# Token-major values by transposing DMA instead of TensorE transposes, in a two-layer hybrid block on one core

## The chip, the cores and the metric

The kernel runs on one core of a Trainium2 chip. The metric is the device time of one execution in microseconds (us); lower is better. The core has five engines with queues of their own: TensorE (PE, matrix products), VectorE (DVE), ScalarE (ACT), GpSimd (POOL) and SyncE (SP), which here issues the DMAs. Each engine takes its instructions in the order in which they were written into its queue.

## The reference

Two layers run over 16 meta tokens and 256 input tokens, width 1024. Each layer mixes tokens in three branches and then applies a convolutional feed-forward block.

```python
def mixer(hn, ...):
    proj = (hn @ w_in).astype(F32)
    rq, rk, rv, rg, hq, hf, hi, hg, dq, dk, dv, mg = jnp.split(proj, offs, axis=-1)
    o_ret = retention(rq, rk, rv, rg, valid, pos)              # 4 heads, values rv, 256 wide
    o_hg = hgrn2(hq, hf, hi, hg, lb, valid)                    # 8 heads, values hi, 128 wide
    o_da = diff_attention(dq, dk, dv, lam_p, subln_g, ...)     # 8 heads, values dv, 128 wide
    branches = jnp.stack([o_ret, o_hg, o_da], axis=2)
    y_b = jnp.einsum('blnc,ncd->blnd', branches, w_branch)
    return jnp.sum(jax.nn.sigmoid(mg) * y_b, axis=2) @ w_out

h = h + mixer(rms_norm(h, g1), ...)
h = h + conv_ffn(rms_norm(h, g2), ...)      # twice, then a final rms_norm of h[:, PAD:]
```

What matters here: in each branch the values (rv, hi, dv) are multiplied from the left by a token-by-token matrix, so that product contracts over tokens.

## The kernel before, in words

**Layout.** Activations lie feature-major: 128 features on the partitions, the 272 tokens (T) along the free dimension. A product of the weight stream makes a pair of feature tiles, `[128, 2, 272]`, in PSUM (tile `main`, two buffers). Weights come as 404 chunks of eight 128x128 float32 tiles. For each chunk SP issues a load into `wraw` (three buffers), ScalarE rounds it to `whi` and VectorE subtracts to get `wlo` (four buffers each). One weight tile then takes three matmuls on TensorE: hi x hi, hi x lo, lo x hi (L912 to L914).

**Order of the weight stream.** `ORDER` lists the pairs of one layer. The pairs of values stand in it like this: `hi` 0 and 1 early, then, after `rg`, `rq` and `rk`, `hi` 2 and 3 and `rv` 0 to 3 directly behind one another, then `dv` 0 and 1, and later `dv` 2 and 3. The heads of a branch are spread as small TensorE work between the main matmuls.

**Values.** A pair of values is feature-major, and the heads need it with tokens on the partitions. `values` (L1378) evacuates the pair from PSUM to a tile `vsrc` on ScalarE (or, before the norm is folded in, on VectorE). `to_tokens` (L948) turns the first 256 tokens: four TensorE transposes into a PSUM tile `vt` of the tag `bank`, then two ScalarE copies from there into the token-major tile (`vt` for hi and dv, `rvt` for rv). The last 16 tokens are copied by GpSimd into `tails` and turned separately for all heads in `tail_tokens`. The heads (`ret_tail` L1000, `ret_head` L1015, `hg_outputs`, `da_head`) then multiply with the token-major tiles; in the profile these are the groups `ro<-wts,rvt`, `ho<-at,vt` and `do<-wts,vt`.

**Who sets the order.** Nothing is issued as it is written. Every operation is handed to `_Plan` with a cost and a due time (`plan.key`); `order` simulates the engines with those costs, the number of buffers of each tag, 0.4 us between engines and 2 us for a DMA to land, and emits one fixed order for each engine. Costs are formulas in `_Engine`; for a GpSimd copy of n elements a partition

```python
cost = self.fixed + self.each * n      # pool: 0.04, 0.85e-3
cost += 1.6e-3 * n                     # pool, except memset
```

A weight load is due `LEAD` = 6 us ahead of its matmuls (L40, L632). `_span` (L383) tells which range of a tile an operation touches. `plan.queue(first, last)` adds an edge: `first` comes after `last`. `SLOTS` (L39) is the number of buffers of the tag `slot`, each 4 x 272 float32 wide, which hold most intermediate blocks, the token-major values among them. The tag `vsrc` has two buffers, the tag `acc` in PSUM has two.

Nearly all small operations are recorded through one helper, so most profile rows have its line, L604; they are told apart by their tiles.

Of the kernel before, what the change touches and what calls it, by code (L numbers as in the profile page):

```python
# [12 lines left out]
F32 = mybir.dt.float32  # L13
F32R = mybir.dt.float32r
U8 = mybir.dt.uint8
AF = mybir.ActivationFunctionType
ALU = mybir.AluOpType
PSUM = bass.MemoryType.PSUM
# [2 lines left out]
P = 128  # L21
# [3 lines left out]
T = META + SEQ  # L25
# [10 lines left out]
TAIL = T - 2 * P  # L36
BANK = 512
CHUNK_TILES = 8
SLOTS = 14  # L39
LEAD = 6.0  # L40
MARGIN = 12.0
EARLY = 12.0
# [313 lines left out]
class _Plan:  # L356
# [5 lines left out]
    SWITCH = 1.3  # L362
    SETS = {AF.Exp: "le", AF.Ln: "le", AF.Silu: "silu", AF.Sigmoid: "sigmoid"}

# [18 lines left out]
    def _span(self, ap):  # L383
        step = ap.ap[0][0]
        lo = ap.offset % step
        hi = lo + 1 + sum((n - 1) * abs(s) for s, n in ap.ap[1:])
        if ap.tensor.name in self.psum:

            lo, hi = lo // BANK * BANK, -(-hi // BANK) * BANK
        return ap.tensor.name, lo, hi  # L390

    def add(self, engine, run, cost, outs, ins, func=None):
# [216 lines left out]
class _Weights:  # L609
# [13 lines left out]
    def next(self):  # L623
        c, i = divmod(self.used, CHUNK_TILES)
        self.used += 1
        if i == 0:
# [7 lines left out]
            for p in range(pieces):  # L634
# [5 lines left out]
                for first, outer, inner, dims in _boxes(*mine):  # L640
                    src = self.part(raw, (p * n + first) * P, inner * P, P, outer, inner)
                    to_hi, to_lo = (self.part(t, *x, outer, inner) for t, x in zip((hi, lo), dims))
                    self.act.activation(to_hi, src, AF.Copy)
                    self.dve.tensor_tensor(out=to_lo, in0=src, in1=to_hi.bitcast(F32), op=SUB)
# [19 lines left out]
def _trace(ctx, tc, plan, a, depth, probe):  # L664
    nc = tc.nc
    act = _Engine(plan, nc.scalar, "act", 0.094, 0.833e-3)
    dve = _Engine(plan, nc.vector, "dve", 0.068, 1.042e-3)
    pe = _Engine(plan, nc.tensor, "pe", 0.0, 4 / 2400)
    pool = _Engine(plan, nc.gpsimd, "pool", 0.04, 0.85e-3)
    sync = _Engine(plan, nc.sync, "sp", 0.06, 4 / 360e3)  # L670
# [3 lines left out]
    wp = ctx.enter_context(tc.tile_pool(name="wp", bufs=3))  # L674
    sp = ctx.enter_context(tc.tile_pool(name="sp", bufs=SLOTS))
    gp = ctx.enter_context(tc.tile_pool(name="gp", bufs=3))
    tp = ctx.enter_context(tc.tile_pool(name="tp", bufs=2))
# [6 lines left out]
    def new(pool_, shape, dt, tag, bufs, name):  # L684
        serial[0] += 1
        return plan.tile(pool_, shape, dt, tag, bufs, f"{name}_{serial[0]}")

    def fixed(shape, name, dt=F32):
        return new(cp, shape, dt, name, 1, name)

    def slot(name, dt=F32):
        return new(sp, [P, 4 * T], dt, "slot", SLOTS, name)

    def slot4(name, dt=F32):
        return slot(name, dt).rearrange("p (a t) -> p a t", a=4)
# [4 lines left out]
    def temp(cols, tag, bufs=2):  # L700
        return new(tp, [P, cols], F32, tag, bufs, tag)

    def temp2(tag, bufs=2):
        return temp(2 * T, tag, bufs).rearrange("p (a t) -> p a t", a=2)

    def bank(name):
        return new(bp, [P, 512], F32, "bank", 2, name)

    def acc_bank(name):
        return new(bp, [P, 512], F32, "acc", 2, name)  # L710

    def tt(out, x, y, op):
        dve.tensor_tensor(out=out, in0=x, in1=y, op=op)
# [7 lines left out]
    def pair(t, n=2):  # L721
        return t.unsqueeze(1).to_broadcast([t.shape[0], n, t.shape[1]])
# [19 lines left out]
    ident = const[:, C_IDENT : C_IDENT + P]  # L742
    masks = fixed([P, 5 * 64], "masks", U8)
    lev = masks[:, : 2 * 64]
# [37 lines left out]
    def parameters():  # L782
# [4 lines left out]
        tt(e, raw, pair(mx), SUB)  # L787
        act.activation(e, e, AF.Exp)
        tt(sm, e[:, 0], e[:, 1], ADD)
# [11 lines left out]
        dve.tensor_reduce(out=sl, in_=pr, axis=mybir.AxisListType.X, op=ADD)  # L801
        act.activation(sl, sl, AF.Exp)
        for li in range(DEPTH):
# [7 lines left out]
    def rsqrt(out, ms, scale=1.0):  # L811

        act.activation(out, ms, AF.Ln, bias=eps, scale=scale)
        act.activation(out, out, AF.Exp, scale=-0.5)

# [108 lines left out]
    def evacuate(out, ps):  # L924
        factor = pair(rstd[:, T - ps.shape[2] :])
        if norm.folded:
            act.activation(out, ps, AF.Copy)
        elif norm.adds is pool and norm.pairs == 1:

            act.activation(out, ps, AF.Copy)  # L930
            plan.key += 2.0
            pool.tensor_tensor(out=out, in0=out, in1=factor, op=MUL)
        else:
            tt(out, ps, factor, MUL)
# [12 lines left out]

    def to_tokens(src, vt, e):  # L948

        pt = bank("vt").rearrange("p (f c e) -> p f c e", f=2, c=2)  # L950
        for f in range(2):
            for c in range(2):
                pe.transpose(pt[:, f, c, :], src[:, f, c * P : (c + 1) * P], ident)
        for f in range(2):
            act.activation(vt[:, :, e + f * P : e + (f + 1) * P], pt[:, f], AF.Copy)

    def tail_tokens(tails):

# [6 lines left out]
    def inverse(r, sq, n):  # L965

        pool.partition_all_reduce(r, sq, P, ReduceOp.add)
        rsqrt(r, r, 1.0 / n)
# [11 lines left out]
    for li in range(depth):  # L980
# [16 lines left out]
        st = {}  # L997


        def ret_tail():  # L1000

            q, k = (st[n][:, :, 2 * P :].unsqueeze(1).to_broadcast([P, 2, 4, TAIL]) for n in ("rq", "rk"))
            ks = temp(P, "tw")
            twice = lambda t: t.rearrange("p (e h t) -> p e h t", e=2, h=4)
            pool.tensor_copy(twice(ks), k)
            s1 = bank("s1")[:, :P]
            pe.matmul(twice(s1), ks, q, start=True, stop=True)
            w = temp(P, "tw")
            tt(w, s1, const[:, C_DECT : C_DECT + P], MUL)
            o = acc_bank("ro")[:, :P]  # L1010
            pe.matmul(o, st["rvs"], w, start=True, stop=True)
            st["ro"] = temp(P, "tw")
            act.activation(st["ro"], o, AF.Copy)

        def ret_head(hd):  # L1015
            q, k, vt, gate = st["rq"], st["rk"], st["rvt"], st["rg"]
            if hd == 0:
                st["dec"] = slot4("dec")
                sync.dma_start(st["dec"].rearrange("p h t -> p (h t)"), a["dec"])
            dec = st["dec"][:, hd, :]  # L1020

            s1 = bank("s1")
            a1 = temp(T + P + TAIL, "wts")
            parts = ((0, t0, t0, dec[:, t0:]), (P, P, T, dec[:, : P + TAIL]))
            for k0, q0, at, _ in parts:
                pe.matmul(s1[:, at : at + T - q0], k[:, hd, k0 : k0 + P], q[:, hd, q0:], start=True, stop=True)
                plan.hold(a1)
            for _, q0, at, by in parts:
                tt(a1[:, at : at + T - q0], s1[:, at : at + T - q0], by, MUL)
            os = [acc_bank("ro") for _ in range(2)]  # L1030
            sq = temp2("sum", 1)
            for e in range(2):
                o = os[e]
                ec = slice((hd * 2 + e) % 4 * P, (hd * 2 + e) % 4 * P + P)
                v = vt[(hd * 2 + e) // 4]
                pe.matmul(o[:, t0:T], v[:, 0, ec], a1[:, t0:T], start=True, stop=False)
                pe.matmul(o[:, P:T], v[:, 1, ec], a1[:, T : T + P + TAIL], start=False, stop=True)
            for e in range(2):
                i = (e * 4 + hd) * TAIL
                tt(os[e][:, 2 * P : T], os[e][:, 2 * P : T], st["ro"][:, i : i + TAIL], ADD)  # L1040
            for e in range(2):
                act.activation(sq[:, e, t0:], os[e][:, t0:T], AF.Square)
            tt(sq[:, 0, t0:], sq[:, 0, t0:], sq[:, 1, t0:], ADD)
            r = temp(T, "hr")
            inverse(r[:, t0:], sq[:, 0, t0:], 2 * P)
            for e in range(2):
                g = gate[:, hd * 2 + e, t0:]
                y = temp(T, "ho")[:, t0:]
                tt(y, os[e][:, t0:T], r[:, t0:], MUL)
                tt(g, y, g, MUL)  # L1050
# [326 lines left out]

        def values(ps, vt, e):  # L1378

            src = temp2("vsrc")  # L1380
            evacuate(src, ps)
            plan.key += 2.0
            to_tokens(src, vt, e)
            return src
# [57 lines left out]
        for name, j in ORDER:  # L1442
# [4 lines left out]
            elif name in ("+hga", "+hgb"):  # L1447
                b = "ab".index(name[3])
# [3 lines left out]
            elif name in ("+daa", "+dab"):  # L1452
                b = "ab".index(name[3])
# [7 lines left out]
            elif name[0] == "*":  # L1461
# [4 lines left out]
                else:  # L1466
                    t = st["rg" if n == "b0" else "hg"]
# [4 lines left out]
            two = slice(2 * (j % 2), 2 * (j % 2) + 2)  # L1472
            both = slice(2 * j, 2 * j + 2)
            if name in BASE:
                lo = 0 if name in FULL else t0
# [17 lines left out]
                elif name in ("dq", "dk"):  # L1493
                    t = block(f"{name}{j // 2}")
# [3 lines left out]
                elif name == "rv":  # L1498
# [3 lines left out]
                    src = values(ps, st["rvt"][j // 2], (j % 2) * 2 * P)  # L1502
# [4 lines left out]
                elif name in ("hi", "dv"):  # L1507
                    n = name[0] + "v"
                    b = j // 2
# [5 lines left out]
                    src = values(ps, st[f"{n}t{b}"], (j % 2) * 2 * P)  # L1515
# [6 lines left out]
                else:  # L1522
                    t = block(f"{name}{j // 2}")
# [21 lines left out]
            elif name == "wo":  # L1545
                hi, lo = st["yhi"], st["ylo"]
# [8 lines left out]
            elif name == "fi":  # L1555
# [10 lines left out]
                c = temp2("two_b")  # L1566
# [8 lines left out]
                c = c[:, :, first:]  # L1575
# [6 lines left out]
            else:  # L1582
                hi, lo = st["ghi"], st["glo"]
# [35 lines left out]
```

## Time and profile before

| | |
|---|---|
| median of 3 runs | 1308.54 us (1308.46 to 1308.67) |
| profiled execution, its own time | 1308.31 us |
| its span, first to last instruction | 1306.5 us |
| granted TensorE clock | 0.999 |
| DMA | 219.06 MB, mean 168 GB/s |

In a group's row stand the line, the engine, the operation, what it writes and reads, the shapes and the count; behind the first bar the busy time in us and the mean ns of one; behind the second the idle time of the engine before it and what ended that. In a row of waits stand who waited for whom, the us in total, how many times and the longest. Timeline rows begin with the start and the length in us.

### The profile page before, as it was taken

To read this page: it belongs to the slowest core of one execution; us is meant where nothing else is said; L and a number is where in the kernel's file an instruction comes from. 1 tells how busy PE (TensorE), PEld (TensorE's weight loads), DVE (VectorE), ACT (ScalarE), POOL (GpSimd) and SP (SyncE) were. 2 spreads that over 40 slices of the span, in tenths; PEclk is the share of its full clock that TensorE was granted. 3 is DMA by queue.
4 is the path that set the end of the run, shared out by engine and by line. 5 is a ranking of instruction groups with operands and counts; after the bars stand their busy time and mean duration, and the time that the engine had idled before them with its cause. 6 is when DMAs were issued, how large, how long until landed. Compare 5 with 4: busy or idle time off the path is not lost.

```text
span 1306.5 us, 28679 instructions
## 1 busy us (share of the span) xinstructions
PE 1294.6 (99%) x11774; PEld 1265.6 (97%) x11774; DVE 958.4 (73%) x1589; ACT 800.5 (61%) x1328; POOL 168.6 (13%) x204
## 2 busy tenths in 40 slices
PE   9999999999999999999999999999999999999998
PEld 9999999999999999999999999999999999999986
DVE  7675777698586789886575767876985867898843
ACT  6846454756576567666456564657565765776643
POOL 5001111222122020000030011012130220200000
PEclk9999999999999999999999999999999999999999
DMA  7644543443534545555555445444445445465553
GB/s 271 200 148 161 169 156 130 162 146 123 184 136 158 181 156 178 189 167 185 175 177 188 164 148 177 148 147 160 146 144 180 139 162 202 145 208 196 200 189 111
DMA packets 60755, 219.06 MB, mean 168 GB/s; under 512 B 6864, under 2 KB 6992, under 8 KB 60624
## 3 DMA queue, kind: packets, MB, share of 16 engines
q1 hardware_dynamic: 60336, 216.71, 49.0%
q8 instruction: 92, 1.51, 0.5%
q10 hardware_dynamic: 288, 0.52, 0.1%
q14 instruction: 39, 0.32, 0.1%
HBM read 216.16 MB, written 1.05 MB: 166 GB/s over the span
## 4 chain that ended last, share of the span: by engine, by line
PE 92%; DVE 5%; issue 1%; ACT 1%; DMA 0%; SPq 0%; DVEq 0%; ACTq 0%
PE main L912 27%; PE main L914 27%; PE main L913 26%; PE fo L1420 2%; PE fo L1419 2%; PE fo L1418 2%; DVE two_b L604 1%; PE lev L1096 1%; DVE two_a L604 1%; DVE wlo L604 1%; PE ds L1280 1%; PE vt L604 1%; PE ro L604 1%; PE ho L604 1%; PE do L604 1%
## 5 line engine op out<-in xcount | busy, mean ns | idle before, releaser
L912 PE MATMUL main<-xh,whi 128*128 128x272 f32 (+1 forms) x2368 | 682.0, 288 | 0.0
L913 PE MATMUL main<-xl,whi 128*128 128x272 f32 (+1 forms) x2368 | 672.5, 284 | 1.5 <-DVE xl L604 1.5
L914 PE MATMUL main<-xh,wlo 128*128 128x272 f32 (+1 forms) x2368 | 673.1, 284 | 0.9 <-DVE wlo L604 0.5
L604 DVE TENSOR_TENSOR wlo<-wraw,whi 128x1024 fp32r<-128x1024 f32 (+1 forms) x411 | 501.9, 1227 | 202.9 <-ACT whi L604 202.2
L604 ACT ACTIVATE whi<-wraw 128x1024 fp32r<-128x1024 f32 (+1 forms) x411 | 427.6, 1043 | 244.5 <-PE main L913 167.1
L914 PEld LDWEIGHTS main<-xh,wlo 128*128 128x128 f32 x2368 | 445.8, 188 | 2.7 <-DVE wlo L604 2.7
L913 PEld LDWEIGHTS main<-xl,whi 128*128 128x128 f32 x2368 | 446.1, 188 | 2.2 <-DVE xl L604 1.9
L912 PEld LDWEIGHTS main<-xh,whi 128*128 128x128 f32 x2368 | 446.1, 188 | 1.0
L604 DVE SCALAR_TENSOR_TENSOR two_b<-main,small,two_b 128x256 f32<-128x256 f32 (+2 forms) x144 | 65.3, 486 | 24.8 <-ACT two_b L604 23.1
L604 POOL PARTITION_ALL_REDUCE hr<-hsq x36 | 67.5, 1886 | 117.0 <-ACT hsq L604 116.2
L604 POOL TENSOR_TENSOR y<-h,rstd 128x272 f32<-128x272 f32 x32 | 34.6, 1112 | 318.1 <-ACT rstd L604 318.1
L604 ACT ACTIVATE two_b<-main,small 128x272 f32<-128x272 f32 (+1 forms) x72 | 37.3, 566 | 24.3 <-PE main L914 23.3
L912 PE MATMUL main<-ghi,whi 128*128 128x272 f32 x176 | 51.0, 290 | 0.0
L913 PE MATMUL main<-glo,whi 128*128 128x272 f32 x176 | 50.6, 287 | 0.0
L914 PE MATMUL main<-ghi,wlo 128*128 128x272 f32 x176 | 50.3, 286 | 0.0
L604 POOL COPY tails<-vsrc 128x32 f32<-128x32 f32 x32 | 10.1, 330 | 225.0 <-ACT vsrc L604 224.9
L912 PE MATMUL main<-b0hi,whi 128*128 128x272 f32 (+1 forms) x128 | 37.9, 296 | 0.0
L912 PE MATMUL main<-b1hi,whi 128*128 128x272 f32 (+1 forms) x128 | 37.8, 296 | 0.0
L912 PE MATMUL main<-yhi,whi 128*128 128x272 f32 (+1 forms) x128 | 36.4, 284 | 0.0
L914 PE MATMUL main<-yhi,wlo 128*128 128x272 f32 (+1 forms) x128 | 36.4, 284 | 0.0
L913 PE MATMUL main<-b1lo,whi 128*128 128x272 f32 (+1 forms) x128 | 36.3, 284 | 0.0
L914 PE MATMUL main<-b1hi,wlo 128*128 128x272 f32 (+1 forms) x128 | 36.3, 284 | 0.0
(236 smaller groups left out, 1915.9 us busy)
## 6 DMA issues: line engine op xcount, KB each, us to landing
wraw<-in_w SPq DMA_DIRECT2D x402, 512.0 KB, 3.3
h<-in_h SPq DMA_DIRECT2D x4, 272.0 KB, 5.3
dec<-in_dec SPq DMA_DIRECT2D x2, 544.0 KB, 4.2
wraw<-in_w SPq DMA_DIRECT2D x4, 256.0 KB, 4.5
const<-in_const SPq DMA_DIRECT2D x1, 937.0 KB, 6.1
gain<-in_gl SPq DMA_DIRECT2D x1, 512.0 KB, 5.5
out<-y ACTq DMA_DIRECT2D x2, 256.0 KB, 3.0
out<-y SPq DMA_DIRECT2D x2, 256.0 KB, 2.9
```

The costliest lines, as they stand in the source:

```text
L604: self.plan.add(self.name, lambda: f(*args, **kw), cost, outs, ins, args[2] if method == "activation" else None)
L912: nc.tensor.matmul(o, wh, hi, start=first, stop=False)
L913: nc.tensor.matmul(o, wh, lo, start=False, stop=False)
L914: nc.tensor.matmul(o, wl, hi, start=False, stop=last)
L1096: nc.tensor.matmul(o, keys, x, start=True, stop=True)
L1280: nc.tensor.matmul(ss[m][:, at : at + nk], q[half, hd, q0 : q0 + P], k[half, hd, :nk], start=True, stop=True)
L1418: nc.tensor.matmul(o, gh, wh, start=False, stop=False)
L1419: nc.tensor.matmul(o, gl, wh, start=False, stop=False)
L1420: nc.tensor.matmul(o, gh, wl, start=False, stop=end)
```

## The change

`to_tokens` no longer uses TensorE, PSUM or ScalarE. It views the float32 values as pairs of 16-bit halves. Two GpSimd copies part the halves into two planes of 128 x 512 (tile `apart`), two DMAs on SP's queue with `transpose=True` turn the four 128x128 blocks of each plane (tile `turned`), and two GpSimd copies join the halves in the token-major tile. Both new tiles are of the tag `vsrc`, which gets four buffers instead of two; `SLOTS` goes from 14 to 13. `_span` learns to count 16-bit views in float32 units. An edge makes the first value matmul of each half of a retention head come after the ScalarE copy of `ret_tail`. The transposes of the last 16 tokens (`tail_tokens`) stay as they are.

```diff
-SLOTS = 14
+SLOTS = 13
...
+        if ap.dtype == U16:
+            lo, hi = lo / 2, hi / 2
         return ap.tensor.name, lo, hi
...
     def to_tokens(src, vt, e):
 
-        pt = bank("vt").rearrange("p (f c e) -> p f c e", f=2, c=2)
-        for f in range(2):
-            for c in range(2):
-                pe.transpose(pt[:, f, c, :], src[:, f, c * P : (c + 1) * P], ident)
-        for f in range(2):
-            act.activation(vt[:, :, e + f * P : e + (f + 1) * P], pt[:, f], AF.Copy)
+        def planes(name):
+            return new(tp, [P, 4 * T], U16, "vsrc", 4, name)[:, : 8 * P].rearrange("p (i x) -> p i x", i=2)
+
+        apart, turned = planes("apart"), planes("turned")
+        halves = lambda t, i: t.bitcast(U16).rearrange("p a (x two) -> p a x two", two=2)[:, :, :, i]
+        for i in range(2):
+            pool.tensor_copy(apart[:, i].rearrange("p (c f x) -> p c f x", c=2, f=2),
+                             halves(src[:, :, : 2 * P], i).rearrange("p f (c x) -> p c f x", c=2))
+        for i in range(2):
+            sync.dma_start(turned[:, i].rearrange("p (b x) -> p b x", x=P), apart[:, i], transpose=True)
+        for i in range(2):
+            pool.tensor_copy(halves(vt[:, :, e : e + 2 * P], i), turned[:, i].rearrange("p (c x) -> p c x", c=2))
...
             act.activation(st["ro"], o, AF.Copy)
+            st["rot"] = plan.ops[-1]
...
                 pe.matmul(o[:, t0:T], v[:, 0, ec], a1[:, t0:T], start=True, stop=False)
+                plan.queue(plan.ops[-1], st["rot"])
...
-            src = temp2("vsrc")
+            src = temp2("vsrc", 4)
             evacuate(src, ps)
```

More of the change, by code (lines that the diff above doesn't have):

```diff
@@ L15 @@
 U8 = mybir.dt.uint8
+U16 = mybir.dt.uint16
 AF = mybir.ActivationFunctionType
```

## The prediction

> **What bounds the kernel now.** I read the page of the profile first: span, busy times, the chain that ended last.
>
> ```profile
> span 1306.5 us, 28679 instructions
> PE 1294.6 (99%) x11774; PEld 1265.6 (97%) x11774; DVE 958.4 (73%) x1589; ACT 800.5 (61%) x1328; POOL 168.6 (13%) x204
> PE 92%; DVE 5%; issue 1%; ACT 1%; DMA 0%; SPq 0%; DVEq 0%; ACTq 0%
> ```
>
> TensorE is busy through 99% of the span and is 92% of the chain. A microsecond taken off TensorE is therefore a microsecond off the end, as long as nothing that feeds it comes late. VectorE has a quarter of the span free, GpSimd nearly all of it. Next, the waits, first of TensorE alone, then of ScalarE's weight conversion:
>
> ```profile
> PE wt L1306 <- DVE two_a L604: 1.6, 4, 0.5
> PE main L913 <- DVE xl L604: 1.5, 2, 1.1
> PE warm L604 <- POOL eps L604: 1.0, 1, 1.0
> PE do L604 <- DVE tw L604: 0.8, 1, 0.8
> PE main L914 <- DVE wlo L604: 0.5, 2, 0.3
> ACT whi L604 <- PE main L913: 167.1, 141, 3.0
> ACT whi L604 <- DMA wraw<-in_w: 17.2, 14, 3.4
> ```
>
> TensorE hardly waits, and after its warm-up it waits for VectorE. The conversion of raw weights (whi, wlo) stood 141 times because TensorE had not yet freed one of its four buffers and only 14 times for a load. So the weights usually run ahead as far as their buffers let them, and that is the cover for much of what follows.
>
> **TensorE's gain.** The change removes 24 groups of four transposes (four pairs each of hi, rv and dv in two layers). One group in the timeline of TensorE (columns: start, length), then the groups of its kind, and ScalarE's evictions behind them:
>
> ```profile
> 160.14 0.29 PE L913 MATMUL main<-xl,whi 128*128 128x272 f32 x1
> 160.26 0.29 PE L914 MATMUL main<-xh,wlo 128*128 128x272 f32 x1
> 160.39 0.60 PE L604 MATMUL vt<-const,vsrc 128*128 128x128 f32 x4
> 160.74 0.37 PE L912 MATMUL main<-xh,whi 128*128 128x272 f32 x1
> 160.95 0.29 PE L913 MATMUL main<-xl,whi 128*128 128x272 f32 x1
> ...
> L604 PE MATMUL vt<-const,vsrc 128*128 128x128 f32 x96 | 15.7, 276 | 0.0
> L604 ACT ACTIVATE vt<-vt 128x256 f32<-128x256 f32 x32 | 10.8, 381 | 3.1 <-PE vt L604 2.6
> L604 ACT ACTIVATE rvt<-vt 128x256 f32<-128x256 f32 x16 | 5.3, 382 | 6.0 <-PE vt L604 6.0
> ```
>
> The 276 ns of one transpose overlap, so I go by starts. From 160.26 to 160.95 pass 0.69 us, where two ordinary steps (0.125 us, as from 160.14 to 160.26) take 0.25: the group costs 0.44 us. From its start to the next main matmul it is 0.35; the other 0.09 is lost in switching, and stays where other small TensorE work stands beside the group. So 24 groups are worth between 24 x 0.35 = 8.4 and 24 x 0.44 = 10.6 us. Most groups stand between main matmuls, so I take 10.0. ScalarE loses 10.8 + 5.3 = 16.1 us of evictions; it isn't the bound, so that counts for nothing.
>
> **GpSimd's copies.** Each group gets four copies of 512 16-bit elements a partition, 96 in all; no such copy is in the trace. The nearest rows (instructions on one tile; min/median/max ns):
>
> ```profile
> L604 POOL COPY dt<-two_a x32: 197/198/1129, 292.8 to 1047.6; 128x16 f32<-128x16 f32 x32
> L604 POOL COPY tw<-rk x2: 289/540/792, 171.6 to 824.2; 128x128 f32<-128x128 f32 x2
> L604 POOL COPY tails<-vsrc x32: 204/212/1052, 74.2 to 991.0; 128x32 f32<-128x32 f32 x32
> L604 POOL TENSOR_TENSOR y<-h,rstd x32: 757/972/1764, 21.6 to 1128.7; 128x272 f32<-128x272 f32 x32
> ```
>
> By minima, 112 elements more cost 92 ns, 0.82 ns each; 512 elements cost 197 + 496 x 0.82 = 604 ns. The upper end goes by the two-input y row: 757 x 512 / 272 = 1.42 us. I take 0.60, because these are copies with one input; that they are 16-bit with a stride of two is what could move it. GpSimd gets 96 x 0.60 = 58 us more, and has room.
>
> The cost is not GpSimd's own time. The maxima above, four to five times the minima, have a partner on VectorE. Eight GpSimd instructions in a row, what VectorE did meanwhile, and wlo overall:
>
> ```profile
> 475.24 8.47 POOL L604 TENSOR_TENSOR y<-h,rstd 128x272 f32<-128x272 f32 x8 [66.64 <-ACT rstd L604]
> 476.14 1.70 DVE L604 TENSOR_TENSOR wlo<-wraw,whi 128x1024 fp32r<-128x1024 f32 x1 [0.23 <-ACT whi L604]
> 478.51 1.77 DVE L604 TENSOR_TENSOR wlo<-wraw,whi 128x1024 fp32r<-128x1024 f32 x1 [0.67 <-ACT whi L604]
> L604 DVE TENSOR_TENSOR wlo<-wraw,whi x411: 418/1224/2189, 5.8 to 1290.6; 128x1024 fp32r<-128x1024 f32 x132, 128x512 fp32r<-128x512 f32 x4, 128x256 fp32r<-128x256 f32 x1
> ```
>
> Beside them wlo takes 1.70 and 1.77 us instead of 1.22, and the eight take 8.47 instead of 8 x 0.757 = 6.1. Both engines pay: they take turns. The Trainium skill, "SBUF — State Buffer", section "Who interferes with whom", states the rule: a VectorE instruction with two SBUF inputs and a GpSimd instruction that reads SBUF share a read port, held for a whole instruction, and the later one stands still. The trace agrees (1.70 against 1.22), and the rule speaks against this change, since wlo is such an instruction.
>
> So I charge VectorE with every copy in full, 0.60 us, as the upper end, and nothing as the lower. Where has it no room for that? Busy time by stretch:
>
> ```profile
> core 0: us, PE busy (x) PEld busy (x) DVE busy (x) ACT busy (x) POOL busy (x), PEclk, DMA share, GB/s
> 73.00:91.00 18.00, 18.00 (x378) 17.25 (x376) 13.17 (x22) 10.27 (x21) 0.51 (x3) 1.00 0.43 148
> 155.00:202.00 47.00, 47.00 (x754) 45.74 (x753) 35.07 (x64) 28.16 (x55) 6.44 (x9) 1.00 0.50 170
> 333.00:352.00 19.00, 19.00 (x157) 19.00 (x156) 10.39 (x10) 12.72 (x22) 2.02 (x8) 1.00 0.52 177
> 805.00:862.00 57.00, 57.00 (x841) 55.70 (x840) 45.61 (x80) 31.79 (x59) 4.78 (x10) 1.00 0.48 163
> ...
> 484.00:512.00 28.00, 27.26 (x217) 26.61 (x216) 27.86 (x53) 20.96 (x37) 0.00 (x0) 1.00 0.39 134
> ```
>
> The second and fourth stretches hold six groups in a row (the last two of hi, four of rv). There 24 copies want 14.5 us, and VectorE has 11.9 and 11.4 us free: 2.6 + 3.1 = 5.7 us too much. Stretches with two groups want 4.8 us and have 4.8 (first) to 8.6 free. When VectorE is full, TensorE does notice: in the last stretch VectorE works 27.86 of 28 us and TensorE idles 0.74. The weight buffers absorb a part, so between 0 and 5.7 I take 3.0 us.
>
> **The DMAs.** There are 48 more, two a group, on SP's queue; each waits for a GpSimd copy, and the weight loads are queued behind it. None is in the trace; its nearest rows are:
>
> ```profile
> wraw<-in_w SPq DMA_DIRECT2D x402, 512.0 KB, 3.3
> h<-in_h SPq DMA_DIRECT2D x4, 272.0 KB, 5.3
> q1 hardware_dynamic: 60336, 216.71, 49.0%
> L604 SPq DMA_DIRECT2D wraw<-in_w x406: 327/328/716, 1.6 to 1283.7; - x136
> ```
>
> A plane has 128 KB. By these rows it takes 0.33 us of issue and lands 3.3 to 5.3 us later; the engines that move data are half idle. Two planes delay a weight load by under 1 us of issue plus the wait for a copy, against loads meant to start 6 us ahead (LEAD): nothing on the path. The Trainium skill, "VectorE: DVE Perf Modes", section "The three transpose paths", gives 1309 ns for a 128x128 16-bit block by DMA and 390 ns on TensorE, and advises TensorE where PSUM will do. By it eight blocks in turn take 10.5 us a group, an estimate, beside TensorE's 0.44 here; no run so far shows a transposing DMA.
>
> Are the values late? They were turned long before they were used (start of first and last):
>
> ```profile
> L604 ACT ACTIVATE rvt<-vt x16: 377/383/386, 174.6 to 852.3; 128x256 f32<-128x256 f32 x16
> L604 PE MATMUL ro<-wts,rvt x64: 284/332/395, 209.3 to 894.8; 128*128 128x144 f32 x32, 128*128 128x272 f32 x16, 128*128 128x258 f32 x16
> ```
>
> From 174.6 to 209.3 there are 35 us. The new path takes 4 x 0.60 for the copies, up to 0.85 us before each (1052 - 204 of tails) and a landing of at most 5.3 after 0.66 of issue: 11.8 us. So latency costs nothing. The four vsrc buffers serve three tiles a group; a third group needs them two spacings later (47 / 6 x 2 = 15.7 us), also longer than 11.8. The joining copies wait on GpSimd for the landing, with the heads' reductions queued behind them, and ScalarE's hr behind those. One slot tile less costs nothing: along the old program's order of issue I count at most 12 held of 14. The new edge (retention's value matmuls after the copy of ro) splits one burst of small TensorE work in each layer: 2 x 0.09 = 0.2 us.
>
> **Sum.** The profiled execution took 1308.31 us (span 1306.5), 0.23 under the median of 1308.54. 1308.31 - 10.0 + 3.0 + 0.2 = 1301.5 profiled, 1301.7 as a median. Its own range is 1297.9 (all 10.6, nothing given back) to 1306.0 (8.4 gained, 5.9 given back).
>
> **Rivals.**
> - *VectorE becomes the bound in the two long stretches; slower.* All 48 copies there hold VectorE up, nothing is absorbed, and a 16-bit copy costs more than 0.60. The loss is 48 d - 23.3 us: it equals the gain of 10.0 at d = 0.69, and at 0.9 it is 19.9, so 1308.5 + 9.9 + 0.2 = 1318.6 us. For it: wlo at 1.77 and the small margin in d. Against it: the copy minima, and the buffers ahead.
> - *SP's queue is held by the transposes; slower.* If SP stands for a whole landing, 2 x 5.3 = 10.6 us a group and 0.9 for its weight loads exceed the spacing of 7.8 by 3.7; six in a row make 22 us, less 6 of lead 16, in both layers 32: 1308.5 + 32 - 10 = 1330.5 us. For it: nothing shows how a transpose is issued, and the skill's 10.5 us would fit. Against it: a load holds SP for 0.33 us whatever its landing.
> - *The gain is eaten.* Joins that stand in GpSimd's queue hold up head reductions, and with them small TensorE work that stands in a fixed order: 24 groups x 0.4 us give the 10 back, 1308.5. For it: GpSimd works in order. Against it: TensorE's waits now are few, and the only one for GpSimd is in its warm-up.
>
> **Numbers.** Forecast 0.55; VectorE 0.20; SP 0.12; eaten 0.13. About 0.2% (2.6 us) is what a measurement of this kernel can tell from no change, so faster means under 1305.9 us. That is nearly all of the forecast and the rare mild outcome of a rival: 0.57. Same 0.13, slower 0.30. The range begins at 1297.5, below the full gain, and ends at 1319, so that it takes in the VectorE rival at 0.9 us and leaves out its worse half and the SP rival.
>
> **What would show it.** The rows of vt on TensorE and 16 us of ScalarE gone; GpSimd busy 58 us more, a copy's minimum near 0.60; VectorE's busy time up by less than 58 us, wlo's mean above 1.23; TensorE's waits for VectorE up by about 3 us, inside 155 to 202 and 805 to 862. Wrong would make it: copies over 0.69 us; a transpose that holds SP for several us and ScalarE's whi waiting for wraw; or TensorE waiting for hr, ro or do.

## The result, and the profile after

| | before | changed |
|---|---|---|
| median | 1308.61 us (1308.05 to 1309.13, 10 runs) | 1305.45 us (1304.03 to 1307.33, 10 runs) |
| ratio | | 0.9974, 95% interval 0.9966 to 0.9983 |
| span of the profiled execution | 1306.5 us | 1303.9 us |

The change is faster by 3.2 us, where 6.8 were forecast (1308.54 - 1301.7). The page of the changed kernel, the lines that answer to those of before:

```profile
span 1303.9 us, 28637 instructions
PE 1285.8 (99%) x11678; PEld 1256.7 (96%) x11678; DVE 986.7 (76%) x1589; ACT 786.7 (60%) x1282; POOL 270.3 (21%) x300
PE 88%; DVE 9%; issue 1%; ACT 1%; DMA 0%; SPq 0%; DVEq 0%; ACTq 0%
```

The 96 transposes are gone and ScalarE is 14 us lighter. But VectorE's share of the chain has gone from 5% to 9%, and it is busy 28 us longer with the same 1589 instructions. TensorE's waits now (who for whom, us in total, times, longest):

```profile
PE lev L1107 <- DVE hf L607: 3.2, 2, 1.7
PE main L916 <- DVE xl L607: 1.5, 2, 1.1
PE ho L607 <- DVE ho L607: 1.4, 2, 0.8
...
PE main L915 <- ACT whi L607: 0.8, 1, 0.8
PE main L917 <- DVE wlo L607: 0.7, 3, 0.3
PE lev L1107 <- DVE tot L607: 0.4, 1, 0.4
PE lev L1107 <- DVE hq L607: 0.4, 1, 0.4
```

New are the waits of `lev` and `ho`, HGRN2's level products and head outputs, for VectorE. The 0.8 for `whi` does not come from the change: that wait ends at 6.06 us, long before the first pair of values. The 1.5 for `xl` was there before. All of TensorE's waits make 11.8 us, against 5.4 before, so 6.4 more (the first expectation below counts 7.7). The new operations themselves, min/median/max ns:

```profile
L607 POOL COPY apart<-vsrc x48: 611/626/1680, 74.0 to 991.6; 128x512 uint16<-128x512 uint16 x48
L607 POOL COPY vt<-turned x32: 767/938/1912, 77.2 to 998.1; 128x512 uint16<-128x512 uint16 x32
L607 POOL COPY rvt<-turned x16: 750/849/1762, 178.6 to 857.6; 128x512 uint16<-128x512 uint16 x16
L607 SPq DMA_TRANSPOSE turned<-apart x48: 1194/1197/2137, 74.7 to 993.2; - x48
DMA to landing us min/median/max: 2.4/4.0/6.0
L607 PE MATMUL ro<-wts,rvt x64: 284/332/393, 212.1 to 894.3; 128*128 128x144 f32 x32, 128*128 128x272 f32 x16, 128*128 128x258 f32 x16
```

The values are still early: the first rvt join starts at 178.6, its first use at 212.1. Where the time went is seen at the largest stall of layer 0. Busy time by engine in the 18 us up to it (PE, PEld, DVE, ACT, POOL), before the change:

```profile
164.00:182.00 18.00, 18.00 (x377) 17.27 (x376) 16.34 (x29) 10.29 (x25) 2.39 (x4) 1.00 0.36 120
```

and after it:

```profile
164.00:182.00 18.00, 15.83 (x298) 15.12 (x297) 17.86 (x24) 9.03 (x17) 13.84 (x16) 1.00 0.64 168
```

The changed kernel's timeline at the end of it, first VectorE, then GpSimd, then TensorE:

```profile
177.08 1.13 DVE L607 TENSOR_TENSOR hq<-hq,tot 128x544 f32<-128x544 f32 x1
178.13 0.57 DVE L607 TENSOR_TENSOR tot<-tot 128x16 f32<-128x16 f32 x1
...
179.35 1.23 DVE L607 TENSOR_TENSOR hf<-hf,tot 128x544 f32<-128x544 f32 x1
...
176.85 1.83 POOL L607 COPY apart<-vsrc 128x512 uint16<-128x512 uint16 x2 [1.51 <-ACT vsrc L607]
178.63 1.42 POOL L607 COPY rvt<-turned 128x512 uint16<-128x512 uint16 x2
...
180.73 0.81 PE L1107 MATMUL lev<-hq,hf 128*32 128x16 f32 x64 [1.49 <-DVE hf L607]
```

The same three VectorE instructions of HGRN2's chain (hq, tot and hf) before the change:

```profile
176.63 0.17 DVE L604 TENSOR_TENSOR tot<-tot 128x16 f32<-128x16 f32 x1
...
176.97 0.72 DVE L604 TENSOR_TENSOR hq<-hq,tot 128x544 f32<-128x544 f32 x1
177.61 0.72 DVE L604 TENSOR_TENSOR hf<-hf,tot 128x544 f32<-128x544 f32 x1
```

In these 18 us VectorE already worked 16.34 before the change; now it works 17.86, with fewer instructions (24 against 29), since hq, tot and hf take 1.13, 0.57 and 1.23 us beside the copies, where they took 0.72, 0.17 and 0.72. The level product on TensorE stands in a fixed order, reaches its place before hf is done and waits 1.49 us, with main matmuls behind it that could run.

### The profile page after: what moved, and what is told of

The parts are those of the page before. It is cut to its first block, busy times and chain, and to the rows that moved or that the text cites. A ratio compares the mean times of both kernels' runs of the same rounds, so it can differ in the third digit from the quotient of the medians.

```text
span 1303.9 us, 28637 instructions
## 1 busy us (share of the span) xinstructions
PE 1285.8 (99%) x11678; PEld 1256.7 (96%) x11678; DVE 986.7 (76%) x1589; ACT 786.7 (60%) x1282; POOL 270.3 (21%) x300
## 4 chain that ended last, share of the span: by engine, by line
PE 88%; DVE 9%; issue 1%; ACT 1%; DMA 0%; SPq 0%; DVEq 0%; ACTq 0%
PE main L915 26%; PE main L917 26%; PE main L916 25%; DVE wlo L607 2%; PE fo L1430 2%; PE fo L1431 2%; PE fo L1429 2%; DVE two_b L607 1%; DVE two_a L607 1%; PE lev L1107 1%; PE ds L1291 1%; PE ho L607 1%; PE ro L607 1%; PE do L607 1%; DVE two_c L607 1%
## 5 line engine op out<-in xcount | busy, mean ns | idle before, releaser
L607 DVE TENSOR_TENSOR wlo<-wraw,whi 128x1024 fp32r<-128x1024 f32 (+1 forms) x411 | 512.0, 1250 | 187.8 <-ACT whi L607 186.6
L607 POOL COPY apart<-vsrc 128x512 uint16<-128x512 uint16 x48 | 40.7, 867 | 145.2 <-ACT vsrc L607 145.0
L607 POOL COPY vt<-turned 128x512 uint16<-128x512 uint16 x32 | 37.0, 1160 | 29.2 <-DMA turned<-apart 29.0
L917 PE MATMUL main<-b0hi,wlo 128*128 128x272 f32 (+1 forms) x128 | 36.4, 284 | 0.0
```

What stands on the lines that cost most here:

```text
L607: self.plan.add(self.name, lambda: f(*args, **kw), cost, outs, ins, args[2] if method == "activation" else None)
L917: nc.tensor.matmul(o, wl, hi, start=False, stop=last)
```

## The experiments

Three theories. A, turn-taking: VectorE stands still for GpSimd's reads, and TensorE's fixed order turns that into stalls. B, uncovered chain: the transposes were work for TensorE between the steps of HGRN2's chain, and without them the chain shows, whatever GpSimd does. C, late loads: the transposing DMAs hold up the weights or the joins.

**Copies without reads** (order on every engine unchanged; the turned values become zeros).

```diff
-            pool.tensor_copy(<out>, <in>)
+            plan.add("pool", lambda: nc.gpsimd.memset(<out>, 0), <the copy's cost>, [<out>], [<in>])
```

> The changed kernel with each of its 96 GpSimd copies replaced by a GpSimd memset of the same output, with the planner told the same costs and dependencies, so that the order on every engine stays. A memset reads nothing from SBUF. The token-major values are then zeros: that part of the computation is left out. Theory A (turn-taking): the 7.7 us of TensorE stalls that the change added come from VectorE standing still for GpSimd's reads; without reads they go, VectorE's busy time falls back from 987 to about 960 us, and the time is about 1305.4 - 6.5 = 1299 us (1298 to 1301). Theory B (uncovered chain): the transposes were filler between steps of HGRN2's chain on VectorE, and with them gone the chain is exposed whatever GpSimd does: the time stays at 1305 (1304 to 1306.5). Theory C (loads late): transposing DMAs delay the weights; they are still there: 1305.

Measured: 1298.11 us (1296.84 to 1298.95), ratio to before 0.9919 (0.9906 to 0.9933). Its page:

```profile
span 1295.6 us, 28628 instructions
PE 1283.2 (99%) x11678; PEld 1255.1 (97%) x11678; DVE 964.1 (74%) x1589; ACT 786.4 (61%) x1282; POOL 224.0 (17%) x300
```

Its memsets, by tile, and the same 18 us by engine:

```profile
L959 POOL MEMSET apart<- x48: 515/526/675, 33.8 to 978.1; 128x512 uint16 x48
L959 POOL MEMSET vt<- x32: 681/698/772, 74.2 to 981.6; 128x512 uint16 x32
```

```profile
164.00:182.00 18.00, 18.00 (x375) 17.27 (x374) 16.66 (x30) 9.37 (x19) 7.64 (x12) 1.00 0.84 163
```

GpSimd writes as much and nearly as long as the copies' minima, but reads nothing: VectorE falls back to 964 us, and in 164 to 182 TensorE is busy throughout. One row of HGRN2's chain shows it: before, in the changed kernel and here (busy us, then mean ns):

```profile
L604 DVE TENSOR_TENSOR hf<-hf,tot 128x544 f32<-128x544 f32 x12 | 8.7, 726 | 4.9 <-PE lev L1096 4.9
L607 DVE TENSOR_TENSOR hf<-hf,tot 128x544 f32<-128x544 f32 x12 | 10.7, 894 | 0.2 <-PE lev L1107 0.2
L607 DVE TENSOR_TENSOR hf<-hf,tot 128x544 f32<-128x544 f32 x12 | 8.7, 727 | 2.3 <-PE lev L1110 2.2
```

B falls: with the same order and no transposes either, TensorE's waits for hf and ho are gone. C falls less firmly here, because a memset waits neither for the evacuation nor for a landing: the first `apart` memset starts at 33.8 us, the first copy at 74.0. A GpSimd that comes late because its joins wait is open for the same reason; against it, ScalarE's waits for GpSimd's head reductions (`hr`) are 6.9 us before and after the change. The run also gives the two terms apart: the change without the copies' reads gains 1308.54 - 1298.11 = 10.4 us, and the reads give back 1305.45 - 1298.11 = 7.3. In the profiled executions the spans are 8.3 us apart; TensorE's waits for VectorE at lev and ho make 5.0 of that (5.4 against 0.4).

This run, the plain DMAs and the two runs with half the memsets keep the order of the changed kernel. In all others the planner makes a new order, and a new order alone can cost several us, as the first kernel under "A planner that knows" shows; their times are weaker evidence for it.

**The copies alone, beside the old transposes** (before's transposes and evictions, plus four copies a group that nobody needs, no DMA).

```diff
+        for i in range(2):
+            pool.tensor_copy(apart[:, i]..., halves(src[:, :, : 2 * P], i)...)
+        for i in range(2):
+            pool.tensor_copy(turned[:, i], apart[:, i])
```

> The kernel before with its TensorE transposes and ScalarE evictions, plus the change's 96 GpSimd copies on scratch tiles that nobody needs (two part the halves, two copy a plane onto another), no transposing DMA, 13 slots, four vsrc buffers. The copies are pure cost. Theory A: the copies' hold on VectorE shows alone, 4 to 8 us over the kernel before: 1312.5 to 1316.5 us. Theories B and C: no more than 1 us over it: 1308 to 1309.6.

Measured: 1312.64 us, ratio 1.0030 (1.0019 to 1.0042): 4.1 us slower than before, at the low end of A's range. Its second copies, by tile, and a row of TensorE's waits:

```profile
L607 POOL COPY turned<-apart x48: 608/612/1613, 75.5 to 998.1; 128x512 uint16<-128x512 uint16 x48
```

```profile
PE lev L1111 <- DVE hf L607: 1.8, 2, 1.3
```

These second copies have both sides dense, and their minimum is 0.608 us, against 0.750 and 0.767 for the joins. Waits of lev for hf appear, with nothing taken off TensorE. Why the copies cost 4.1 us here and 7.3 in the changed kernel was not taken apart: the joins are longer there, the order is another, and the transposes no longer stand between the small work.

**Plain DMAs in place of transposing ones** (same order; values not turned).

```diff
-            sync.dma_start(turned[:, i]..., apart[:, i], transpose=True)
+            sync.dma_start(turned[:, i], apart[:, i])
```

> The changed kernel with the 48 transposing DMAs as plain DMAs of the same bytes between the same tiles; the order on every engine is that of the changed kernel. The token-major values are then not turned: that part of the computation is left out. Theory C (1.2 us of issue on SP and a 4 us landing per transpose make the weights or the joins late): 1302 us or less. Theories A and B: 1305 (1304 to 1306).

Measured: 1304.55 us, ratio 0.9972 (0.9960 to 0.9983), against 0.9974 for the change. The DMAs, by tile:

```profile
L607 SPq DMA_DIRECT2D turned<-apart x48: 465/471/1448, 75.0 to 991.8; - x48
DMA to landing us min/median/max: 1.9/3.6/5.3
```

That a transpose holds SP for 1.20 us instead of 0.47 and lands 0.4 us later costs nothing that can be told from zero. C falls.

**Where the give-back lies** (memsets in half of the groups, same order; `LONG` true, then false).

```diff
+            if LONG != (name == "rv" or (name, j) in (("hi", 2), ("hi", 3))):
+                run = lambda: nc.gpsimd.tensor_copy(out, x)      # else the memset
```

> The changed kernel with GpSimd's copies as memsets (no reads) in the 12 groups of the two six-group stretches alone (last two of hi, four of rv in each layer); the other 12 groups keep their copies; the order on every engine is that of the changed kernel. The values of those 12 groups are zeros. If the give-back of 7.3 us that the full memset kernel took away lies in the long stretches, as the stalls in the trace of the changed kernel have it (2.4 + 3.4 of 8.1 us above the memset kernel's): 1299.2 to 1301 us. If it is spread evenly over the groups: 1301.8.

Measured: 1300.22 us, ratio 0.9938 (0.9926 to 0.9949): 5.2 of the 7.3 us lie in the two six-group stretches.

> The complement: memsets in the other 12 groups (first two of hi, all of dv), copies in the two six-group stretches; same order. By the stalls of the trace 2.2 us go: 1302.5 to 1304.2 us. Spread evenly: 1301.8. If the give-back were all in the long stretches: 1305.4.

Measured: 1304.05 us, ratio 0.9963 (0.9951 to 0.9975): 1.4 us in the other twelve. The two parts make 6.6 of 7.3.

**Copies on ScalarE.**

```diff
-            pool.tensor_copy(<out>, <in>)
+            act.activation(<out>, <in>, AF.Copy)
```

> The changed kernel with all 96 copies of 16-bit halves on ScalarE instead of GpSimd; the transposing DMAs stay. ScalarE gets some 96 x 0.55 = 53 us (787 to 840 of 1300). Theory A (GpSimd's reads hold up VectorE): the stalls go as with the memsets, and this time with the values right: 1298 to 1301 us, VectorE's busy time near 960. Theory B (uncovered chain) and theory C (loads late behind the transposes): 1304 to 1306, since what they name is unchanged. If ScalarE's own queue becomes the late one: whi or the small activations of HGRN2's chain come late, 1302 to 1308.

Measured: 1299.51 us (1298.64 to 1301.11), ratio 0.9934 (0.9920 to 0.9947). Its page, then its copies by tile:

```profile
span 1298.2 us, 28609 instructions
PE 1283.4 (99%) x11678; PEld 1254.8 (97%) x11678; DVE 960.9 (74%) x1589; ACT 838.9 (65%) x1376; POOL 165.8 (13%) x204
```

```profile
L607 ACT ACTIVATE apart<-vsrc x48: 602/616/639, 73.8 to 984.0; 128x512 uint16<-128x512 uint16 x48
L607 ACT ACTIVATE vt<-turned x32: 763/790/806, 77.0 to 989.7; 128x512 uint16<-128x512 uint16 x32
```

The same copies take as long on ScalarE as their minima on GpSimd, never more than 0.81 us, and VectorE is back at 961. Here the copies wait for evacuation and landing as in the changed kernel, so the memsets' lack of such waits is not what removed the stalls for VectorE. This version beats both kernels. Next, ScalarE for part of the copies: by place, then by kind.

```diff
+        move = (ScalarE's copy) if name == "rv" or (name, j) in (("hi", 2), ("hi", 3)) else pool.tensor_copy
```

> The changed kernel with the copies of the two six-group stretches on ScalarE and those of the other 12 groups on GpSimd, all values right; the planner makes a new order. If the place of the give-back is what counts: within 2.5 us of the kernel with all copies on ScalarE (1299.5), 1299.5 to 1302.

Measured: 1300.38 us (1299.39 to 1305.31), ratio 0.9945 (0.9933 to 0.9957): ScalarE for the two long stretches alone gets nearly all of it, as expected.

```diff
-            pool.tensor_copy(halves(vt[:, :, e : e + 2 * P], i), turned[:, i]...)
+            act.activation(halves(vt[:, :, e : e + 2 * P], i), turned[:, i]..., AF.Copy)
```

> The changed kernel with the 48 joining copies on ScalarE and the 48 parting copies on GpSimd. Theory A: about half of the give-back goes, a little more because a join is the longer copy: 1300.5 to 1303 us. Theories B and C: 1304 to 1306.

Measured: 1304.27 us (1301.54 to 1305.38), ratio 0.9967 (0.9954 to 0.9979). Too little against the 1300.5 to 1303 that A expected, and inside the range of B and C. But VectorE's busy time has fallen to 966 us, so little of its hold is left. TensorE's waits, the longest of them in the timeline, and a stretch behind it:

```profile
PE lev L1107 <- issue: 3.3, 2, 2.2
PE lev L1107 <- DVE hf L607: 1.2, 2, 0.6
...
191.30 0.31 PE L1107 MATMUL lev<-hq,hf 128*32 128x16 f32 x8 [2.18 <-issue]
...
191.00:194.00 3.00, 2.70 (x19) 2.66 (x19) 1.49 (x3) 2.85 (x6) 0.00 (x0) 0.50 0.82 313
```

A wait "for issue" has no releaser in the profile. The two waits cost 3.3 us, and the trace grants half the clock for 3.41 us from 190.9, which costs another 1.7: without these 5.0 us the time would be about 1299.3 (an estimate), that of all copies on ScalarE. So in this execution the missing time lies in waits that none of the three theories names. Why they come stays open. In the traces of seven of these kernels there are ten such waits of TensorE, and each ends 1.1 to 1.5 us after a 16 KB packet of the instruction queue has landed (here from 188.44 to 189.82); an execution has 92 such packets. That points to instructions that arrive late, but no run tested it.

**A planner that knows.** First the true durations alone, then turn-taking for all GpSimd reads, then for the new copies alone.

```diff
+            if self.name == "pool" and method == "tensor_copy":
+                cost = 0.19 + 0.83e-3 * n + (0.14 if <strided 16-bit output> else 0.0)
...
+                cost = 1.2 if kw.get("transpose") else self.fixed + self.each * n * outs[0].shape[0]
...
+            if op.port:                      # the second and third kernel
+                t = max(t, port[0])          # and port[0] = t + cost once chosen
```

> The changed kernel, its planner told the durations that the profile shows: 0.62 us for a parting copy and 0.76 for a joining one instead of 1.29, 1.2 us of issue and 2.8 to landing for a transposing DMA instead of 0.79 and 2.0. Nothing else changes. Theory A: the planner still knows nothing of the turn-taking, so the chain is placed as tightly as before: 1303.5 to 1307. If wrong costs alone were the reason: 1299 to 1301.

Measured: 1313.01 us, ratio 1.0037 (1.0024 to 1.0049), a miss for A: 7.6 us slower than with the wrong costs. TensorE's waits:

```profile
PE vm L609 <- POOL tails L609: 3.3, 5, 0.9
PE lev L1109 <- DVE tot L609: 3.3, 2, 2.3
```

A reading that no run tests: the cost of 1.29 us in the changed kernel's plan had acted as a margin, and with the bare 0.62 and 0.76 TensorE's small work stands closer behind GpSimd and VectorE, and waits more. The DMAs' costs were changed in the same run.

> As the kernel with the true costs, and the planner also lets a GpSimd instruction that reads SBUF and a VectorE instruction with two SBUF inputs (or a one-input tensor_scalar or copy from SBUF) run only one after the other; an edge keeps a third group's evacuation behind the first group's DMA, so that the four vsrc buffers don't run out. Theory A: TensorE's small work is now placed where VectorE really is, and most of the stalls go: 1299.5 to 1303 us. Theory B: the chain is exposed by the missing filler, and the planner could already see that: 1304 to 1307.

Measured: 1327.79 us, ratio 1.0143 (1.0129 to 1.0156), a miss. TensorE's longest wait:

```profile
PE lev L1122 <- DVE hf L615: 9.1, 5, 2.3
```

TensorE idles 9.9 us in the two six-group stretches (155 to 215 and 805 to 875 us) and 10.8 us in two stretches of the norm (490 to 530 and 1120 to 1175). So the stalls lie in both places about equally, not mostly at the norm, as the next expectation has it. The third kernel keeps the edge on the evacuation.

> The changed kernel with the true durations in the planner and turn-taking modelled for the 96 new copies alone (the earlier attempt modelled every GpSimd read, and its stalls lay mostly in the norm's stretches around 500 and 1150 us, far from the change). Theory A: small TensorE work placed by where VectorE really is: 1300 to 1304 us. If a fixed order can't be made to fit turn-taking this way: 1306 to 1315.

Measured: 1318.66 us, ratio 1.0081 (1.0067 to 1.0095). A miss as well. Its waits and a stretch by engine have the old place, and more of it:

```profile
PE lev L1122 <- DVE hf L615: 9.8, 5, 2.2
```

```profile
178.00:189.00 11.00, 7.37 (x179) 7.18 (x168) 5.61 (x10) 2.66 (x7) 4.32 (x6) 0.53 0.52 93
```

So a planner with turn-taking in it did not make an order that fits. A expected that it would, so these two do not support A; as their orders are new, they do not tell against the hold on VectorE either. Part of the loss is the clock: it was granted 0.993 and 0.992 in these two profiled executions, against 0.998 in the changed kernel's, which is some 7 and 8 us of 1320 (an estimate). Why the orders fail was not tried.

## Why the prediction was right and wrong

- *TensorE's gain, 10.0 us: right.* The memset kernel measures 10.4, as the net of all that the change does besides the copies' reads.
- *GpSimd's copies, 0.60 us: right for the parting copies* (minimum 0.611), low for the joins (0.750 and 0.767), which write with a stride. The mean of the minima is 0.69, just where the VectorE rival had its turning point. It did not come to that, since the hold falls on both engines: the 96 copies take 93 us instead of 66 by their minima (58 forecast), and VectorE is busy 22.6 us longer than with memsets, a third of 66.
- *The mechanism, turn-taking: right.* In the changed kernel's trace a full wlo takes 1.221 us on average where no GpSimd instruction runs beside it (277 times) and 1.355 where only copies do (50 times); beside memsets alone, in the memset kernel, it takes 1.221 (17 times). The 24 predicated copies `near<-masks,lev`, which read lev from PSUM, are not held: 15 of them have GpSimd copies alone beside them, and their 128x128 form takes 352 ns on average, 354 before the change. Not only two-input instructions are held: the TENSOR_SCALAR `hf<-hf,keep` takes 0.35 us alone and up to 0.87 beside copies. In "SBUF — State Buffer", section "Who interferes with whom", the Trainium skill exempts a GpSimd instruction that only writes SBUF. The trace agrees: with memsets of 0.53 and 0.70 us VectorE's busy time is 964, with copies 987.
- *The give-back, 3.0 us of at most 5.7: this step failed.* It measured 7.3, of which 5.2 in the two long stretches, where the forecast had its 3.0. Two things were wrong in it. The room was averaged over 47 us (11.9 us free), while the chain that TensorE follows sits, at the stall of layer 0, in 18 us with 1.7 us free (18.00 - 16.34). And the buffers that were to absorb a part belong to the weights; the level products have no such lead, and it is there and at the head outputs that TensorE waits. Also, the other stretches were taken as free and cost 1.4 us. Charging every copy in full was too much, as said. That the bound of 5.7 lies near the measured 5.2 is in part luck: with 0.69 us a copy the same sum gives 9.8.
- *The DMAs: no cost, right*, with a term mis-sized: a transpose issues for 1.20 us, not 0.33, and lands in 4.0 (3.3 to 5.3 forecast). The estimate of 10.5 us a group from the Trainium skill's "VectorE: DVE Perf Modes", section "The three transpose paths", does not fit: two planes issue in 2.4 us and land 4.0 us after their issue.
- *Latency, the slots, the vsrc buffers: no cost, right as far as the traces go.*
- *The rivals.* "SP's queue is held" fell with the plain DMAs. "The gain is eaten" through GpSimd's queue did not show: in the changed kernel no new wait of TensorE is for GpSimd. The VectorE rival named the right engine and the right stretches; at 7.3 us it stayed under the gain.
- *The sum.* 10.4 - 7.3 = 3.1 against 10.0 - 3.2 = 6.8: the result lies in the range and on the forecast side, at less than half the forecast size.

## What to carry to other kernels

Before moving copies to an idle GpSimd, look for two-input VectorE instructions beside them (a TENSOR_SCALAR was held here too), and count each copy, as an upper bound, against the chain that VectorE serves. Take the free time from the stretch of that chain, not from an average around it. If ScalarE has room, the copies can go there: VectorE's busy time stayed at 961 us, against 958 before the change.

## What the runs showed of the hardware

TensorE's clock fell to half after a stall far shorter than the half-clocked stretch that followed. In the changed kernel, by stretch (PE busy first, the granted clock after the five engines):

```profile
826.00:834.00 8.00, 5.88 (x162) 5.43 (x161) 7.96 (x12) 3.12 (x7) 5.49 (x6) 0.98 0.76 223
834.00:838.00 4.00, 4.00 (x73) 3.85 (x76) 2.59 (x4) 1.43 (x3) 0.06 (x1) 0.60 0.65 173
```

and in TensorE's timeline:

```profile
832.50 0.73 PE L1107 MATMUL lev<-hq,hf 128*32 128x16 f32 x64 [1.70 <-DVE hf L607]
834.22 0.43 PE L915 MATMUL main<-xh,whi 128*128 128x272 f32 x1
834.45 0.43 PE L916 MATMUL main<-xl,whi 128*128 128x272 f32 x1
```

After a wait of 1.70 us and one burst of 32-wide level products, main matmuls start 0.23 us apart instead of 0.125, and over the 4 us from 834 the clock was granted 0.60: 1.6 us lost on top of the wait. In the stretch shown of the last planner, too, it was granted only 0.53. The kernel with plain DMAs, in the same order, has the wait at this place (1.71 us) and not the drop (1.00 granted), with a span of 1302.3 against 1303.9 us. So such a wait can end in a drop and need not; what decides it is not shown. The Trainium skill, "TensorE: Matmul & The Clock Gate", section "Why this matters for your kernels", warns of idle gaps over about 3 us between matmul bursts. Here the clock fell after one of 1.70 us with thin work behind it.

Not expected either: ScalarE copies strided 16-bit halves as fast as GpSimd (0.616 against 0.626 us), and GpSimd's memsets leave VectorE's wlo at its 1.221 us.
